# Blank idle matmuls, a later request for sixteen columns, and weights loaded by row halves, in the first norm of an encoder block

## The chip, the cores and the metric

The kernel runs on one core of a Trainium2 chip. The metric is device time in microseconds of one launch. The engines of the core: PE is TensorE (PEld its weight loads), DVE is VectorE, ACT is ScalarE, POOL is GpSimd, SP is SyncE, which here only issues DMAs.

## What is computed

One block of a hybrid encoder, in float32: `x` has 1024 tokens of 1024 channels, and 16 learned meta tokens stand ahead of them. The part that matters here is the beginning:

```python
h = jnp.concatenate([meta, x], axis=1)
u = rmsnorm(h, norm_mix)                      # y = x * rsqrt(mean(x*x) + 1e-6) * g
z = jnp.einsum('bld,dn->bln', u, w_in)        # w_in: 1024 x 4112
a, q, k, v, r, lr, ga, gb = jnp.split(z, IN_SPLITS, axis=-1)
log_a = log_sigmoid(lr @ w_gate_up + b_gate) / 16
```

`v` has 512 columns and the low-rank input `lr` has 16. Behind it come a multi-scale pooling mixer, a chunked gated linear attention over 4 heads, a merge by sigmoid gates, an output projection with a residual, a second rmsnorm, a squared-ReLU MLP of width 4096, and a last rmsnorm.

## The kernel before

**Arithmetic.** A product of two float32 matrices is taken as three products of rounded parts: each operand is split into a high part (ScalarE's Copy into the type fp32r) and a low part (VectorE's subtraction). `TH`/`TL` hold the high and low parts of the normed, transposed input, in two halves of 512 tokens; `w1h`/`w1l` and `vw` hold those of weights.

**The order of the work.** TensorE's instructions stand in the order in which the program writes them, everywhere (`manual_schedule` for PE around the whole run). In `start()`, the stage around the change, the order of ScalarE, VectorE and GpSimd is written out too. What lies outside that block on these engines, and SP's queue of DMAs, is ordered by a planner, which may bring instructions forward. Each engine works in order and stops at an instruction whose inputs aren't there.

**The first stage, `start()`.** x is taken in tiles of 128 tokens. SP asks for x's tile 0, the 128x128 identity (`ident`), the norm weights (`g8`), x's tile 1, two blocks of value weights (`fetch_vw(0)`, 512 KB each, into the two `raw` buffers), and tiles 2 and 3. GpSimd asks for the 16 low-rank columns of `w_in` (`lrraw`, L651). Later tiles are asked for when a buffer is free, in `normed()`.

A tile t goes through these steps:

- `squared(t)`, L606: ScalarE squares the tile and sums each row;
- `root(t)`, L608 and L609: ScalarE's Ln and Exp give a first estimate of the inverse root;
- `rest(t)`, L611 to L614 on VectorE (L611 and L616 to L619 on GpSimd from tile 3 on): one step that refines it;
- `normed(t)`, L660: VectorE scales the tile into `us`; then TensorE transposes its eight 128x128 blocks against the identity (L578) into two PSUM banks of four;
- `taken(t)`, twice, one bank each: VectorE multiplies by the norm weights into `ut` (L585), ScalarE makes the high part `th` (L594), and a returned function makes the low part `tl` on VectorE (L595).

`load_vw(0)` splits the value weights: `hi(j)` is ScalarE's high part of block j (L471), `lo(j)` VectorE's low part (L474), `lr()` the high part of the low-rank columns (L478, ScalarE), which returns the low part's function (L479, VectorE). `vw` holds 272 columns for each of 8 row blocks: 256 of values and 16 low-rank. In the kernel before, block j is 128 columns over all 1024 rows, in rows of 512 bytes.

`v_tile(0, t)` is the product of one tile with `vw`: "hh", "lh" and "hl", eight matmuls of 272 columns each (L506), one name for each pair of high and low parts. From tile 2 on the three are interleaved (L255 to L257).

`warm(n)` puts n idle transposes of the identity on TensorE (L668), into a bank that nothing reads; `WARM` holds the three counts. `S["fs"]` is a buffer that the gate stage uses later.

Of the kernel before, what the change touches and what calls it, by code (L numbers as in the profile page):

```python
# [11 lines left out]
ACT = mybir.ActivationFunctionType  # L12
ALU = mybir.AluOpType
AX = mybir.AxisListType

P = 128
D = 1024
SEQ = 1024
META = 16
KT = D // P  # L20
HALF = 512
# [9 lines left out]
NPAIR = DFF // P // 2  # L31
MP = 264
PACE, LEVEL = 1.1, 1.6
WARM = (4, 8, 12)


class Stack:
# [77 lines left out]
def kernel(  # L115
# [84 lines left out]
    def f32(ap):  # L200
        return ap.bitcast(F32)
# [245 lines left out]
    def w_cols(c):  # L447
        return w_in[:, c : c + P].rearrange("(k p) c -> p k c", p=P)
# [11 lines left out]
        return [slice(h * HALF, (h + 1) * HALF) for h in range(2)]  # L460

    def fetch_vw(i):
        return [raw.load(w_cols(C_V + i * 256 + j * P), D).rearrange("p (k c) -> p k c", k=KT) for j in range(2)]

    def load_vw(i, raws=None, parts=False):
        vw, raws = S["vw"][i], raws or fetch_vw(i)
        c = [slice(j * P, (j + 1) * P) for j in range(2)]
        eng = pool if i else dve

        def hi(j):  # L470
            act.activation(vw[:, 0, :, c[j]], raws[j], ACT.Copy)  # L471

        def lo(j):
            eng.tensor_tensor(vw[:, 1, :, c[j]], raws[j], f32(vw[:, 0, :, c[j]]), ALU.subtract)  # L474

        def lr():
            r = S["lrraw"]
            act.activation(vw[:, 0, :, 256:], r, ACT.Copy)  # L478
            return lambda: dve.tensor_tensor(vw[:, 1, :, 256:], r, f32(vw[:, 0, :, 256:]), ALU.subtract)  # L479

        if parts:
            return hi, lo, lr
        for j in range(2):
            hi(j)
            lo(j)
# [101 lines left out]
    def taken(b, t):  # L587

        half, at = t // 4, OFF[t // 4] + (t % 4) * P
        for j in range(2):  # L590
            ut = S["ut"][half, j][:, :, (t % 4) * P : (t % 4 + 1) * P]
            hi, lo = (a[half][:, 4 * j : 4 * j + 4, at : at + P] for a in (TH, TL))
            weighted(ut, b[j], j)
            act.activation(hi, ut, ACT.Copy)  # L594
            yield lambda lo=lo, ut=ut, hi=hi: dve.tensor_tensor(lo, ut, f32(hi), ALU.subtract)  # L595
# [26 lines left out]
    def start():  # L622
        act.preload_act_table_set("natural_log_exp_and_others")
        S["lrtok"] = left.push("lrtok", [P, 16, 16], F32)
        S["lrraw"] = left.push("lrraw", [P, KT, 16], F32)
        S["left_x"] = left.mark()
        xs = left.push("xs", [P, 4, D], F32)
        us = left.push("us", [P, 3, D], F32)
        xm = left.push("xm", [META, D], F32)
        g8 = xm[:KT, :P]  # L630
        mf = left.push("mf", [P, 6, CH], F32)
        S["u2p"] = right.push("u2p", [P, 2, HALF], F32)
        S["fs"] = right.push("fs", [P, 2, HALF], F32)
        S["s3"] = right.push("s3", [P, HALF], F32)
        q = gate_quarters
        q.lead = 1
        for i in range(2):
            q.places[i][0] = right.push(f"rawx{i}", [P, D], F32)
        S["right_ut"] = [right.mark()]
        S["ut"] = {}  # L640
        for half, j in ((0, 1), (1, 0), (1, 1), (0, 0)):
            S["ut"][half, j] = right.push(f"ut{half}{j}", [P, 4, HALF], F32)
            S["right_ut"].append(right.mark())
        S["vw"] = [right.push("vw0", [P, 2, KT, VP], F32R)]
        load = lambda t: nc.sync.dma_start(xs[:, t % 4], x[t * P : (t + 1) * P, :])
        load(0)
        nc.sync.dma_start(ident, ident_in)
        nc.sync.dma_start(g8, norm_mix.rearrange("(k p) -> k p", p=P))
        load(1)
        raws = fetch_vw(0)  # L650
        pool.dma_start(S["lrraw"], w_in[:, C_LR : C_LR + 16].rearrange("(k p) c -> p k c", p=P))  # L651
        load(2)
        load(3)
        m = lambda half, j: tuple(a[half][:, 4 * j : 4 * j + 4, OFF[half] : OFF[half] + HALF] for a in (TH, TL))
        q.x.update({"P1": m(0, 0), "P2": m(0, 1), "P3": m(1, 1)})
        run = S["gate_run"] = q.run()
        def normed(t):

            x_, u = of(t)
            dve.tensor_scalar(u, x_, rs[t], None, ALU.mult)  # L660
            if t < 4:
                load(t + 4)
            return turned(u)

        def warm(n):

            for _ in range(n):
                pe.transpose(idle[:, :P], ident, ident)  # L668

        idle = bank("x")  # L670
        of = lambda t: (xs[:, t % 4], us[:, t % 3])
        nothing = lambda: None
        with tc.manual_schedule(engines={mybir.EngineType.Activation, mybir.EngineType.DVE, mybir.EngineType.Pool}):
            rs, rms, b, leave = {}, {}, {}, None

            def squared(t):
                rms[t] = first_rms(xm if t == 8 else xs[:, t % 4], us[: META if t == 8 else P, t % 3], pool if t > 2 else dve)
                next(rms[t])

            def root(t):  # L680
                next(rms[t])

            def rest(t):
                rs[t] = next(rms[t])

            warm(WARM[0])
            bg = bank("ms")
            pe.transpose(bg[:, :KT], g8, ident[:KT, :KT])
            warm(WARM[1])
            squared(0)  # L690
            root(0)
            rest(0)
            b[0] = normed(0)
            dve.tensor_copy(gcol, bg[:, :KT])
            squared(1)
            root(1)
            lows = [list(taken(b[0], 0))]
            rest(1)
            warm(WARM[2])
            b[1] = normed(1)  # L700
            hi, lo, lr = load_vw(0, raws, True)
            hi(0)
            hi(1)
            lr_lo = lr()
            v0, leave0 = v_tile(0, 0, by_part=True)
            v1, leave = v_tile(0, 1, by_part=True)
            v0("hh")
            for fn in lows[0]:
                fn()
            v0("lh")  # L710
            lows.append(list(taken(b[1], 1)))
            v1("hh")
            for j in range(2):
                lo(j)
            lr_lo()
            v0("hl")
            squared(2)
            root(2)
            rest(2)
            b[2] = normed(2)  # L720
            v1("hl")
            for fn in lows[1]:
                fn()
            v1("lh")
            squared(3)
            root(3)
            rest(3)
            q.load(0, 0)
            squared(4)
            root(4)  # L730
            for t in range(1, 8):
                if t > 1:
                    left_now, leave = leave, v_tile(0, t, True)
                else:
                    left_now = leave0
                if t < 6:
                    b[t + 2] = normed(t + 2)
                if t < 2:
                    q.load(t, 0)
                elif t == 2:  # L740
                    nc.sync.dma_start(xm, meta)
                    q.load(0, 1)
                    q.load(1, 1)
                    nc.sync.dma_start(mf, masks)
                elif t == 7:
                    dve.tensor_scalar(xm, xm, rs[8], None, ALU.mult)
                for fn in left_now:
                    fn()
                if t < 6:
                    rest(t + 3)  # L750
                lows = list(taken(b[t + 1], t + 1)) if t < 7 else []
                if t < 5:
                    squared(t + 4)
                    root(t + 4)
                for fn in lows:
                    fn()
                for n in {5: (0,), 6: (1, 2), 7: (3,)}.get(t, ()):
                    q.prime(n == 0)
            differ((0, 0), (1, 0), (0, 0))
            bm = bank("ms")[:, : 8 * META].rearrange("p (a b) -> p a b", a=8)  # L760
            for i in range(KT):
                pe.transpose(bm[:, i], xm[:, i * P : (i + 1) * P], ident[:META, :META])
            um = us[:, 0, : 8 * META].rearrange("p (a b) -> p a b", a=8)
            for j in range(2):
                weighted(um[:, 4 * j : 4 * j + 4], bm[:, 4 * j : 4 * j + 4], j)
            th, tl = (a[0][:, :, :META] for a in (TH, TL))
            act.activation(th, um, ACT.Copy)
            dve.tensor_tensor(tl, um, f32(th), ALU.subtract)
            pool.tensor_copy(mask, mf)
            differences(run, leave)  # L770
# [1062 lines left out]
```

## Time and profile before

| | us |
|---|---|
| median of 3 runs | 1218.23 (1218.12 to 1218.29) |
| the profiled execution, its time | 1218.34 |
| its span, first to last instruction | 1216.1 |
| TensorE busy in the span | 1198.0 (99%) |
| VectorE / ScalarE / GpSimd busy | 854.6 / 618.5 / 63.0 |
| first TensorE instruction | 4.58 |

A row of the timeline gives start, duration, engine, line, operation, the tile written and the tiles read, shapes and, in brackets, how long the engine stood idle before it and what ended that wait. A row of the chain of waits gives start, duration, engine, tile and line of one piece of the chain that ended last. A row of the view of busy time by stretch gives the stretch, its length, the busy time and instruction count of PE, PEld, DVE, ACT and POOL, TensorE's granted clock, the DMA engines' mean busy share and GB/s. A row of a DMA queue gives packets, MB and the time that its packets took as a share of the 16 engines in the stretch asked for; `q1` is SP's queue and `q0` GpSimd's. A row of a DMA issue ends with KB and the time from issue to landing.

### The profile page before, as it was taken

Reading aid. Unit: us, or ns where it says so; the run is one execution under the profiler, and the core shown is the slowest. Engines: PE = TensorE matmul, PEld = TensorE weight load, DVE = VectorE, ACT = ScalarE, POOL = GpSimd, SP = SyncE. Lnnn points to the kernel's source line nnn. Section 1 sums busy time; section 2 is a strip of 40 time slices with the busy share of each in tenths; the row PEclk is TensorE's granted clock in tenths of the full one; section 3 lists DMA queues with packets and bytes.
Section 4 is the critical chain, followed back from the end, with each engine's and each line's share of the span. In section 5 each row is a group of like instructions: output and inputs, shape, how many; then the busy total and the mean of one; then the engine's idle time right before and its main releaser. Section 6 shows DMA issues by size and latency. Waiting matters only on the chain.

```text
span 1216.1 us, 18370 instructions
## 1 busy us (share of the span) xinstructions
PE 1198.0 (99%) x6818; PEld 997.9 (82%) x6818; DVE 854.6 (70%) x1411; ACT 618.5 (51%) x1103; POOL 63.0 (5%) x100
## 2 busy tenths in 40 slices
PE   7999999999999999999999999999999999999997
PEld 7878888988887778888888888888888888888886
DVE  7996676654556677735897667676675887887686
ACT  7667567322446663324655455454554444444554
POOL 2000000001201126000000000000000000000000
PEclk9999999999999999999999999999999999999999
DMA  8043426146102246741245454344479973333532
GB/s 255 2 113 114 125 77 201 45 153 223 36 19 62 71 144 230 267 149 70 105 139 166 145 165 156 130 162 146 168 239 326 337 241 96 95 98 94 173 96 87
DMA packets 141672, 173.84 MB, mean 143 GB/s; under 512 B 9944, under 2 KB 81392, under 8 KB 141584
## 3 DMA queue, kind: packets, MB, share of 16 engines
q1 hardware_dynamic: 141552, 172.62, 44.0%
q8 instruction: 53, 0.87, 0.3%
q14 instruction: 35, 0.29, 0.1%
q0 software_dynamic: 32, 0.07, 0.1%
HBM read 119.17 MB, written 53.48 MB: 142 GB/s over the span
## 4 chain that ended last, share of the span: by engine, by line
PE 92%; DVE 4%; ACT 2%; issue 1%; DMA 0%; POOL 0%; SPq 0%; ACTq 0%; POOLq 0%; DVEq 0%
PE b_mm L255 11%; PE b_mm L256 11%; PE b_mm L257 11%; PE b_ms L257 9%; PE b_ms L255 9%; PE b_ms L256 9%; PE b_x L256 8%; PE b_x L255 8%; PE b_x L257 8%; PE b_mx L255 1%; PE b_sc L1227 1%; PE b_mx L256 1%; PE b_mx L257 1%; PE b_ms L1505 1%; DVE ut L783 1%
## 5 line engine op out<-in xcount | busy, mean ns | idle before, releaser
L255 PE MATMUL b_mm<-th,w1h 128*128 128x512 f32 (+1 forms) x312 | 117.6, 377 | 1.1 <-DVE c L818 1.0
L256 PE MATMUL b_mm<-tl,w1h 128*128 128x512 f32 (+1 forms) x312 | 115.9, 372 | 0.0
L257 PE MATMUL b_mm<-th,w1l 128*128 128x512 f32 (+1 forms) x312 | 115.9, 371 | 0.0
L255 PE MATMUL b_x<-th,w1h 128*128 128x512 f32 (+1 forms) x240 | 90.8, 378 | 0.0
L256 PE MATMUL b_x<-tl,w1h 128*128 128x512 f32 (+1 forms) x240 | 90.7, 378 | 0.0
L257 PE MATMUL b_x<-th,w1l 128*128 128x512 f32 (+1 forms) x240 | 90.3, 376 | 0.0
L273 ACT ACTIVATE w1h<-raw 128x512 fp32r<-128x512 f32 x96 | 59.5, 620 | 29.0 <-PE b_ms L256 13.7
L274 DVE TENSOR_TENSOR w1l<-raw,w1h 128x512 fp32r<-128x512 f32 x96 | 65.6, 684 | 8.6 <-ACT w1h L273 8.6
L255 PEld LDWEIGHTS b_mm<-th,w1h 128*128 128x128 f32 x312 | 58.6, 188 | 12.5 <-issue 1.9
L273 ACT ACTIVATE w1h<-fs 128x512 fp32r<-128x512 f32 x72 | 45.3, 631 | 44.9 <-PE b_ms L256 30.8
L257 PEld LDWEIGHTS b_mm<-th,w1l 128*128 128x128 f32 x312 | 58.6, 188 | 10.4
L256 PEld LDWEIGHTS b_mm<-tl,w1h 128*128 128x128 f32 x312 | 58.6, 188 | 9.8
L273 ACT ACTIVATE w1h<-bt 128x512 fp32r<-128x512 f32 x44 | 27.8, 632 | 67.1 <-issue 62.7
L274 DVE TENSOR_TENSOR w1l<-fs,w1h 128x512 fp32r<-128x512 f32 x72 | 49.2, 686 | 15.0 <-ACT w1h L273 14.9
L1681 DVE TENSOR_TENSOR bt<-w,w 128x512 f32<-128x512 f32 x80 | 54.7, 684 | 1.6 <-DMA w<-in_w_ff_dram 1.6
L257 PEld LDWEIGHTS b_x<-th,w1l 128*128 128x128 f32 x240 | 45.1, 188 | 8.5
L255 PEld LDWEIGHTS b_x<-th,w1h 128*128 128x128 f32 x240 | 45.1, 188 | 8.4
L256 PEld LDWEIGHTS b_x<-tl,w1h 128*128 128x128 f32 x240 | 45.1, 188 | 8.3
L273 ACT ACTIVATE fxh<-bt 128x512 fp32r<-128x512 f32 x36 | 22.8, 632 | 55.7 <-issue 50.1
L257 PE MATMUL b_ms<-wo,w1l 128*128 128x512 f32 x128 | 49.9, 390 | 0.0
L255 PE MATMUL b_ms<-wo,w1h 128*128 128x512 f32 x128 | 49.8, 389 | 0.0
L256 PE MATMUL b_ms<-wo,w1h 128*128 128x512 f32 x128 | 49.8, 389 | 0.0
(455 smaller groups left out, 3345.2 us busy)
## 6 DMA issues: line engine op xcount, KB each, us to landing
hf_dram<-h SPq DMA_DIRECT2D x112, 256.0 KB, 2.1
raw<-hf_dram SPq DMA_DIRECT2D x112, 256.0 KB, 2.7
w<-in_w_ff_dram SPq DMA_DIRECT2D x64, 256.0 KB, 4.8
raw<-in_w_in_dram SPq DMA_DIRECT2D x24, 512.0 KB, 4.8
raw<-in_w_ff_dram SPq DMA_DIRECT2D x16, 512.0 KB, 4.1
rawx<-in_w_ff_dram SPq DMA_DIRECT2D x16, 512.0 KB, 4.0
xs<-in_x_dram SPq DMA_DIRECT2D x8, 512.0 KB, 5.5
rawx<-in_w_in_dram SPq DMA_DIRECT2D x8, 512.0 KB, 4.4
```

The costliest lines, as they stand in the source:

```text
L255: pe.matmul(ps, ah, bh, start=first and i == 0, stop=False, skip_group_check=more)
L256: pe.matmul(ps, ah, bl, start=False, stop=False, skip_group_check=more)
L257: pe.matmul(ps, al, bh, start=False, stop=last and i == n - 1, skip_group_check=more)
L273: act.activation(hi, a, ACT.Copy)
L274: dve.tensor_tensor(lo, a, f32(hi), ALU.subtract)
L783: dve.tensor_tensor(to_, a_, b_, ALU.subtract)
L1227: pe.matmul(b[to, e, j], kk[r, s], qq[r, s], start=True, stop=True, tile_position=(e * CH, u * CH))
L1505: pe.transpose(b[j][:, i], u[:, (4 * j + i) * P : (4 * j + i + 1) * P], ident)
L1681: dve.tensor_tensor(bt, w, S["w2"][q[3:]][:, i], ALU.add if q[2] == "+" else ALU.subtract)
```

## The change

The idle work on TensorE is a float32 matmul of a blank tile with itself: the first 128 columns of `S["fs"]`, which VectorE sets to zero. It needs no load. `WARM` has four counts: ten ahead of the transposition of the norm weights, four behind it, two ahead of tile 1's transposes, and three behind the splits of the value weights.

The low-rank columns are asked for by GpSimd behind a copy of one column of x's tile 1 into the same buffer, so behind that tile's landing.

The value weights come as two row halves of 512 rows by 256 columns (rows of 1 KB), and `hi(j)`, `lo(j)` work on row blocks 4j to 4j+3. This holds for the second set (`load_vw(1)`) too.

The second half of tile 0's `taken` (L585 and L594) moves behind tile 1's `rest` and `normed` on VectorE and behind `hi(0)` on ScalarE; `lr()` stands ahead of `hi(1)`.

```diff
-WARM = (4, 8, 12)
+WARM = (10, 4, 2, 3)
...
     def fetch_vw(i):
-        return [raw.load(w_cols(C_V + i * 256 + j * P), D).rearrange("p (k c) -> p k c", k=KT) for j in range(2)]
+        rows = lambda j: w_in[j * HALF : (j + 1) * HALF, C_V + i * 256 : C_V + (i + 1) * 256]
+        return [raw.load(rows(j).rearrange("(k p) c -> p k c", p=P), D).rearrange("p (k c) -> p k c", k=4) for j in range(2)]
...
-        c = [slice(j * P, (j + 1) * P) for j in range(2)]
+        at = lambda n, j: vw[:, n, 4 * j : 4 * j + 4, :256]
...
-            act.activation(vw[:, 0, :, c[j]], raws[j], ACT.Copy)
+            act.activation(at(0, j), raws[j], ACT.Copy)
...
-            eng.tensor_tensor(vw[:, 1, :, c[j]], raws[j], f32(vw[:, 0, :, c[j]]), ALU.subtract)
+            eng.tensor_tensor(at(1, j), raws[j], f32(at(0, j)), ALU.subtract)
...
         raws = fetch_vw(0)
-        pool.dma_start(S["lrraw"], w_in[:, C_LR : C_LR + 16].rearrange("(k p) c -> p k c", p=P))
...
+        blank = S["fs"][:, 0, :P]
+        dve.memset(blank, 0.0)
+
         def warm(n):
 
             for _ in range(n):
-                pe.transpose(idle[:, :P], ident, ident)
+                pe.matmul(idle[:, :P], blank, blank, start=True, stop=True)
...
+            pool.tensor_copy(S["lrraw"][:, 0, :1], xs[:, 1, :1])
+            pool.dma_start(S["lrraw"], w_in[:, C_LR : C_LR + 16].rearrange("(k p) c -> p k c", p=P))
             warm(WARM[0])
...
-            lows = [list(taken(b[0], 0))]
+            parts = taken(b[0], 0)
+            lows = [[next(parts)]]
             rest(1)
             warm(WARM[2])
             b[1] = normed(1)
             hi, lo, lr = load_vw(0, raws, True)
             hi(0)
+            lows[0] += parts
+            lr_lo = lr()
             hi(1)
-            lr_lo = lr()
+            warm(WARM[3])
```

## Prediction

> **What bounds the kernel now.** The profile page's first line, then the view of busy time by stretch, for two stretches.
>
> ```profile
> span 1216.1 us, 18370 instructions
> ```
>
> ```profile
> 24.00:1180.00 1156.00, 1151.88 (x6578) 958.65 (x6577) 814.95 (x1327) 585.29 (x1030) 57.47 (x82) 1.00 0.44 142
> 1180.00:1216.10 36.10, 28.37 (x126) 23.13 (x124) 24.19 (x54) 16.48 (x37) 0.00 (x0) 0.93 0.26 88
> ```
>
> From 24 us to 1180 us TensorE (first busy column) is idle for 1156.00 - 1151.88 = 4.1 us. What starts sooner or later ahead of 24 us shifts all of that and comes out in the total nearly one for one, and the stake is small. The change works ahead of 24 us, so I read that stretch in the chain of waits:
>
> ```profile
> 2.07 6.04 DMA xs<-in_x_dram
> 8.13 1.16 ACT us L606 x2
> ...
> 10.86 0.75 DVE us L660
> ...
> 13.45 1.23 ACT th L594 x2
> ...
> 16.18 1.14 ACT us L606 x2
> ...
> 19.72 0.76 DVE us L660
> ...
> 22.52 0.39 PE b_mm L257
> ```
>
> The end is set by x's second tile (asked for at 2.07, landed at 8.1), its norm, then from 13.45 by ScalarE, in order: split of tile 1 (L594), squares of tiles 2 and 3 (L606), the norm of tile 3 on GpSimd, VectorE, and TensorE from 22.5 on. So one start decides: **L594 at 13.45**. The timeline has what stands before it (rows of TensorE, VectorE and ScalarE, in this order):
>
> ```profile
> 7.59 1.91 PE L578 MATMUL b_ms<-ident,us 128*128 128x128 f32 x8
> ...
> 11.66 1.09 PE L578 MATMUL b_ms<-ident,us 128*128 128x128 f32 x8 [0.77 <-DVE us L660]
> ...
> 8.69 0.69 DVE L585 TENSOR_TENSOR ut<-b_ms,small 128x512 f32<-128x512 f32 x1 [1.21 <-PE b_ms L578]
> 9.54 0.69 DVE L585 TENSOR_TENSOR ut<-b_ms,small 128x512 f32<-128x512 f32 x1 [0.16 <-PE b_ms L578]
> 10.15 0.14 DVE L611 TENSOR_SCALAR small<-small 128x1 f32<-128x1 f32 x1
> 10.41 0.22 DVE L613 SCALAR_TENSOR_TENSOR small<-small 128x1 f32<-128x1 f32 x1
> ...
> 11.52 1.29 DVE L595 TENSOR_TENSOR tl<-ut,th 128x512 fp32r<-128x512 f32 x2
> 12.73 1.28 DVE L585 TENSOR_TENSOR ut<-b_ms,small 128x512 f32<-128x512 f32 x2
> ...
> 9.31 0.29 ACT L608 ACTIVATE small<-small 128x1 f32<-128x1 f32 x1
> 9.64 0.20 ACT L609 ACTIVATE small<-small 128x1 f32<-128x1 f32 x1
> ...
> 10.80 1.99 ACT L471 ACTIVATE vw<-raw 128x1024 fp32r<-128x1024 f32 x2
> 12.70 0.29 ACT L478 ACTIVATE vw<-lrraw 128x128 fp32r<-128x128 f32 x1
> 13.45 1.23 ACT L594 ACTIVATE th<-ut 128x512 fp32r<-128x512 f32 x2 [0.46 <-DVE ut L585]
> ```
>
> Eight transposes take 1.91 us at 7.59 and 1.09 at 11.66: TensorE's pace changes in between. VectorE waits 1.21 us for the first group, and from 10.86 it is full. L594 waits for tile 1's L585 at 12.73; the low-rank columns (L478) are split at 12.70 without a wait.
>
> **The change, part by part.**
>
> *Idle matmuls.* A blank tile needs one memset. Rows of the timeline (VectorE's first, TensorE's first), then pieces of the chain of waits:
>
> ```profile
> 0.81 0.07 DVE L1191 MEMSET metab<- 128x16 f32 x1 [0.81 <-PEq L1822]
> 4.58 1.11 PE L668 MATMUL b_x<-ident 128*128 128x128 f32 x4 [4.58 <-DMA ident<-in_ident_dram]
> ```
>
> ```profile
> 37.19 0.45 PE b_ms L578 x4
> 37.66 0.70 DVE ut L585
> ...
> 388.25 1.03 PE b_m L1316 x32
> ```
>
> After a memset of that size TensorE starts near 1.1 instead of 4.58, 3.5 us sooner. The eight transposes that end at 9.50 are the last at the lower pace, 4.9 us after TensorE's first work, so the pace should now rise by 6.0, if TensorE stays busy. Full f32 matmuls on a 128x128 tile aren't in the trace: L1316's smaller ones take 1.03/32 = 0.03 us each, the idle transposes 1.11/4 = 0.28; between those ends I take 0.28, the row of the same shape. Ten then end at 1.1 + 2.8 = 3.9, and four behind the identity (4.58) and the norm weights well before tile 0's transposes at 7.5. At the fast pace VectorE follows 0.47 behind four transposes (37.19 to 37.66), so L585 starts at 7.59 + 0.47 = 8.06 instead of 8.69: **-0.6**, bounds 0 (the hole of 0.7 us or more until the identity lands keeps the pace down) and -0.6. The two and three further matmuls lie in TensorE's wait for L660.
>
> *Order on VectorE.* The second half of tile 0's L585 moves behind L660 of tile 1. L660 then waits only for L613's inputs, and the half's own 0.69 is worked off after it. A gain only if x's second tile comes early enough; on its own it costs.
>
> *The low-rank request.* Rows of DMA, by stretch: GpSimd's queue in 3.5:4.5, 4.5:6 and 6:7, then the landings of x's second tile, of the low-rank columns and of the second value-weight block (issued 2.94), and rows of GpSimd, and one of VectorE, in the timeline:
>
> ```profile
> q0 software_dynamic: 16, 0.06, 65.2%
> q0 software_dynamic: 13, 0.01, 1.9%
> q0 software_dynamic: 3, 0.00, 0.2%
> ...
> xs<-in_x_dram SPq DMA_DIRECT2D x1, 512.0 KB, 6.0
> lrraw<-in_w_in_dram POOLq DMA_DIRECT2D x1, 64.0 KB, 5.7
> raw<-in_w_in_dram SPq DMA_DIRECT2D x1, 512.0 KB, 8.6
> ```
>
> ```profile
> 1.27 1.10 POOL L651 DMA_DIRECT2D lrraw<-in_w_in_dram  x1 [0.44 <-issue]
> ...
> 17.77 1.29 DVE L595 TENSOR_TENSOR tl<-ut,th 128x512 fp32r<-128x512 f32 x2
> ...
> 18.02 0.48 POOL L616 TENSOR_TENSOR small<-small 128x1 f32<-128x1 f32 x1
> ...
> 20.87 0.19 POOL L617 TENSOR_TENSOR small<-small 128x1 f32<-128x1 f32 x1
> ```
>
> In 3.5 to 4.5 the low-rank columns held 65% of all 16 engines for 1 us, just ahead of x's second tile. Without them that tile lands 0.65 sooner: 8.13 - 0.65 = 7.48, bounds 8.13 (the value weights take the room) and 7.0.
>
> The path by VectorE: squares end 1.15 after landing, 8.65; L608 8.68, L609 9.01, end 9.21; L585 (first half) 8.06 to 8.74; L613 9.24, L660 0.45 later (10.41 to 10.86), 9.69; second half of L585 0.66 later (10.86 to 11.52), 10.35; two L595 0.69 later, 11.04; tile 1's L585 1.21 later (11.52 to 12.73), 12.25; L594 0.72 later (12.73 to 13.45): **12.97**, i.e. -0.48. With the tile at 7.0 the first L585's end, 8.75, limits (L611 to L660 0.71): -0.71. With it at 8.13 (L613 9.87): +0.15.
>
> What was moved must still land. GpSimd now waits for x's tile, runs a one-column copy (0.19, up to 0.48 beside VectorE's L595), then the request: 7.48 + 0.3 = 7.8. Behind it on GpSimd stands nothing that is needed before the norm of tile 3 (L616 at 18.02). The copy is one more reader of the tile's buffer, but the next load into that waits for L660 anyway. From issue to landing it took 5.7, the data packets being over by 5.0 (3.7 after the issue); 13 of 16 closing packets were out by 6.0, three later. Bounds 3.7 and 5.7; I take 5.0, since the last three belong to engines that lagged in the stretch where x's tile was also late, and the request now begins when that tile is whole. Landing 12.8. And L478 has moved ahead of the second L471, so ScalarE, in order, holds behind it: the second L471, both L594, the squares of tiles 2 and 3. From L478's start to L594 it is 0.26 + 0.95 = 1.21 (12.70 to 12.96; half of L471's pair). So L594 at 12.8 + 1.21 = 14.01: **+0.56**, in place of the -0.48 by VectorE; the later of the two counts. With 3.7 the landing is 11.5, L594 12.7 by this path, and VectorE's 12.97 stands. With 5.7: 13.5, +1.26. The landing costs from 11.8 on and is worse than before from 12.24 on.
>
> By the Trainium skill, "DMA: Bandwidth & Descriptors", section "Anatomy of one DMA — SWDGE (gpsimd) path", a request from GpSimd costs about 2.0 us plus bytes over 436 GB/s, 2.15 for these 64 KB; with the 1.10 of the issue that would land at 11.05 and the wait would vanish. The row here (5.7) speaks against it.
>
> *Value weights by row halves.* Same bytes in 1 KB rows instead of 512 B. The second block landed at 2.94 + 8.6 = 11.54 before; its L471 is now due near 12 at the earliest (second half of L585 to 11.04, its L594, then L478), so it isn't last. TensorE's first products can begin on half the rows, but what ends their stage is the low part of the low-rank columns on VectorE, as before: nothing. SP spends less on descriptors; x's later tiles aren't in the chain. The second set of value weights is fetched far inside the stretch where TensorE is full: nothing; uncovered, a block's landing would show, 8.6 us at the worst row here.
>
> *Sum.* 1218.34 (the profiled execution: span 1216.1 and 2.2 around it) + 0.56 = 1218.9; the median of the runs, 1218.23, lies 0.11 lower: **1218.8**.
>
> **Rivals.**
> 1. *The columns land in time* (by 11.8). For it: data packets over 3.7 us after the issue. Against: SP's queue, by then, is fuller (row below, 7 to 9 us: 122.6%) than in the stretch where the 5.7 was measured. -0.48 (to -0.71): 1217.8.
>
> ```profile
> q1 hardware_dynamic: 1222, 0.65, 122.6%
> ...
> 13.04 1.27 PE L506 MATMUL b_mm<-vw,th 128*128 128x272 f32 x8 [0.29 <-ACT vw L478]
> ```
>
> 2. *It doesn't do what it says*: pace and x's tile unchanged. Landing 8.13 + 0.3 + 5.0 = 13.4, L594 at 14.6, +1.2: 1219.4.
> 3. *GpSimd is slowed by VectorE while it writes the request* — the slower side. L616 took 0.48 beside VectorE's L595, L617 0.19 beside its L585: 2.5 times. In the run before the request was written with VectorE idle; now VectorE is busy from 8.06 on, though with L585 first, which weighs against it. 1.10 and the 1.2 to the first data packet (2.37 to 3.5) become 2.8 and 3.0, landing 14.5 (the issue alone) to 16.3: +2.3 to +4.1, about +3.0: 1221.2. It leaves the 0.2% from a landing at 14.64 on, +2.4. The Trainium skill, "SBUF — State Buffer", the box on the "DVE blocks DMA" trap, says that VectorE in a two-port mode locks GpSimd out of writing descriptors; the rows here show slower GpSimd operations and no locked request.
> 4. *The planner sets another order later*: L1191, of a much later stage, ran at 0.81, so order outside the written-out part is its own choice. At most the 4.1 us that TensorE idles, either way: 1214 to 1222.
> 5. *TensorE falls back to the lower pace* with fewer idle matmuls after 9 us: three passes like the one at 13.04 above, 1.2 each, would take double: +3.5: 1221.7.
>
> **How the numbers follow.** Forecast (late by under 1.5 us): 0.42. Rival 1: 0.27. Rival 2: 0.08. Rival 3: 0.10, 0.08 of it beyond +2.4. Rival 4: 0.10, of which 0.04 faster and 0.04 slower by over 0.2%. Rival 5: 0.03. A measurement of this kernel tells about 0.2%, 2.4 us, from no change. Faster 0.04; slower 0.08 + 0.04 + 0.03 = 0.15; within 0.81. The range takes forecast, rivals 1 and 2 and the near parts of 3 and 4 (0.81): from 1217.4 (-0.71, with 0.1 for runs) to 1220.7; the forecast's own is 1218.3 to 1219.7.
>
> **What would show it.** TensorE at work from about 1.1 us; tile 0's transposes in about 1.1 us, not 1.91; L585 at 8.1; x's squares of tile 1 at 7.5; GpSimd's request near 7.8; a wait on ScalarE in front of L478 named after the columns' DMA, of about 1 us; L594 near 14.0. No wait there and L594 at 13.0 means rival 1; a request row well over 1.10 is rival 3; a shift that appears only behind 60 us is rival 4. The forecast is wrong if L594's shift and the end's shift differ by over 0.5 us.

## The result and the profile after

The changed kernel takes **1220.45 us** (median of 14 runs, 1220.09 to 1221.77) against 1218.20 for the kernel before on the same chip (14 runs, 1217.74 to 1218.65): ratio 1.0019, 95% interval 1.0012 to 1.0027, so 2.25 us slower. The profiled execution, of which the rows below are, is the longest of the 14: 1221.77, that is 3.43 above the profiled one of before.

The changed kernel's page and its view of busy time by stretch:

```profile
span 1219.7 us, 18402 instructions
```

```profile
24.00:1180.00 1156.00, 1151.58 (x6591) 959.31 (x6591) 814.29 (x1325) 585.52 (x1032) 58.25 (x84) 1.00 0.44 142
```

TensorE is idle for 4.42 us between 24 and 1180 us, against 4.1 before: hardly anything changed there. The 3.6 us by which the span grew lie ahead of it. The chain of waits of the changed kernel:

```profile
2.04 5.72 DMA xs<-in_x_dram
...
7.82 0.20 POOL lrraw L689
8.02 0.29 issue
8.30 6.52 DMA lrraw<-in_w_in_dram
...
14.91 0.32 ACT vw L479
...
15.27 7.09 PE b_mm L507 x32
22.36 0.87 PE b_ms L579 x8
```

Of VectorE's and ScalarE's norm work nothing is left in it. It runs from x's second tile to GpSimd's copy, the request, 6.52 us of transfer, the split of the columns, and then TensorE's products. Most lines of the changed kernel are numbered one higher: L594 is L595 now, L478 is L479, L471 is L472, L585 is L586, L578 is L579, L606 is L607, L506 is L507. Its timeline (TensorE, VectorE, ScalarE, GpSimd, in this order):

```profile
1.05 4.11 PE L671 MATMUL b_x<-fs 128*128 128x128 f32 x20 [1.05 <-DVE metab L1199]
7.52 1.09 PE L579 MATMUL b_ms<-ident,us 128*128 128x128 f32 x8 [1.11 <-DVE us L660]
11.72 0.83 PE L671 MATMUL b_x<-fs 128*128 128x128 f32 x6
15.27 2.22 PE L507 MATMUL b_mm<-vw,th 128*128 128x272 f32 x8 [2.72 <-ACT vw L479]
...
8.21 0.69 DVE L586 TENSOR_TENSOR ut<-b_ms,small 128x512 f32<-128x512 f32 x1 [0.67 <-PE b_ms L579]
12.64 1.28 DVE L586 TENSOR_TENSOR ut<-b_ms,small 128x512 f32<-128x512 f32 x2
...
7.79 1.06 ACT L607 ACTIVATE us<-xs 128x1024 f32<-128x1024 f32 x1 [1.56 <-DMA xs<-in_x_dram]
14.91 0.31 ACT L479 ACTIVATE vw<-lrraw 128x128 fp32r<-128x128 f32 x1 [2.91 <-DMA lrraw<-in_w_in_dram]
15.13 1.04 ACT L472 ACTIVATE vw<-raw 128x1024 fp32r<-128x1024 f32 x1
16.07 1.14 ACT L595 ACTIVATE th<-ut 128x512 fp32r<-128x512 f32 x2
...
7.82 0.19 POOL L689 COPY lrraw<-xs 128x1 f32<-128x1 f32 x1 [6.74 <-DMA xs<-in_x_dram]
8.30 1.11 POOL L690 DMA_DIRECT2D lrraw<-in_w_in_dram  x1 [0.30 <-POOL lrraw L689]
```

Each of the intended steps is there: TensorE at work from 1.05, tile 0's transposes in 1.09, L586 at 8.21, x's second tile a little sooner (7.79). VectorE begins tile 1's L586 at 12.64, where it began at 12.73 before. But ScalarE stands for 2.91 us in front of L479, and L595, whose start decided the end before, starts at 16.07 instead of 13.45: **+2.62**. The end moved by 3.6, which is 1.0 more than L595, and the chain above doesn't pass through L595 any more: from L479 it goes by TensorE's products. The view of busy time by stretch, last columns TensorE's granted clock, DMA share and GB/s, shows what happens there:

```profile
12.00:14.00 2.00, 0.55 (x5) 0.36 (x4) 1.97 (x4) 0.00 (x0) 0.00 (x0) 1.00 1.04 330
14.00:15.00 1.00, 0.00 (x0) 0.00 (x0) 1.00 (x1) 0.09 (x1) 0.00 (x0) 0.85 0.98 339
15.00:21.00 6.00, 5.73 (x25) 5.73 (x26) 3.73 (x9) 5.87 (x13) 0.98 (x2) 0.50 0.64 171
```

While ScalarE waits TensorE has nothing either (0.55 us of work from 12 to 14, none from 14 to 15), and its clock falls to 0.50 for the six microseconds in which the first products run: eight take 2.22 us instead of 1.27.

### The profile page after: what moved, and what is told of

Its sections match the earlier page's. It is cut to its first block, busy times and chain, and to the rows that moved or that the text cites. A ratio compares the mean times of both kernels' runs of the same rounds, so it can differ in the third digit from the quotient of the medians.

```text
span 1219.7 us, 18402 instructions
## 1 busy us (share of the span) xinstructions
PE 1200.9 (98%) x6832; PEld 1002.1 (82%) x6832; DVE 855.5 (70%) x1412; ACT 618.6 (51%) x1103; POOL 63.4 (5%) x101
## 4 chain that ended last, share of the span: by engine, by line
PE 90%; DVE 5%; ACT 2%; DMA 1%; issue 1%; SPq 0%; POOL 0%; ACTq 0%; DVEq 0%
PE b_mm L255 11%; PE b_mm L256 11%; PE b_mm L257 11%; PE b_ms L256 9%; PE b_ms L255 9%; PE b_ms L257 9%; PE b_x L256 8%; PE b_x L255 8%; PE b_x L257 8%; PE b_mx L255 1%; PE b_sc L1235 1%; PE b_mx L256 1%; PE b_mx L257 1%; PE b_mm L507 1%; DVE w1l L274 1%
## 5 line engine op out<-in xcount | busy, mean ns | idle before, releaser
L274 DVE TENSOR_TENSOR w1l<-fs,w1h 128x512 fp32r<-128x512 f32 x72 | 49.3, 686 | 15.0 <-ACT w1h L273 14.9
```

Source lines behind the costliest of these rows:

```text
L274: dve.tensor_tensor(lo, a, f32(hi), ALU.subtract)
```

## The experiments

All times stand beside runs of the kernel before on the same chip: eleven runs of each version, fourteen of the change and seven of "request on ScalarE's queue". In the table, the shift of tile 1's high part (L594 or L595) and of the span are those of one profiled execution each, against 13.45 and 1216.1.

| run | median (range), us | kernel before | ratio, 95% interval | shift of tile 1's high part | shift of span |
|---|---|---|---|---|---|
| the change | 1220.45 (1220.09-1221.77) | 1218.20 | 1.0019 [1.0012, 1.0027] | +2.62 | +3.6 |
| request early | 1218.37 (1217.62-1218.84) | 1218.35 | 0.9998 [0.9990, 1.0007] | +0.33 | +0.4 |
| request on SP | 1217.32 (1217.04-1217.65) | 1218.35 | 0.9992 [0.9983, 1.0001] | -0.66 | -0.7 |
| only request late | 1219.75 (1218.94-1221.31) | 1218.35 | 1.0012 [1.0003, 1.0021] | +1.51 | +2.0 |
| long filler | 1220.19 (1219.67-1221.93) | 1218.35 | 1.0017 [1.0008, 1.0026] | +2.20 | +1.8 |
| pace kept | 1219.81 (1219.47-1220.67) | 1218.31 | 1.0012 [1.0003, 1.0021] | +2.14 | +2.3 |
| columns split later | 1218.55 (1218.08-1220.11) | 1218.31 | 1.0003 [0.9994, 1.0012] | +0.66 | +2.0 |
| request on ScalarE's queue | 1221.80 (1220.22-1223.73) | 1218.31 | 1.0027 [1.0016, 1.0038] | +2.64 | +2.7 |
| queue held back | 1217.67 (1217.15-1218.20) | 1218.49 | 0.9994 [0.9985, 1.0002] | -0.50 | -0.8 |
| idle matmuls only | 1217.63 (1217.28-1219.51) | 1218.31 | 0.9998 [0.9989, 1.0006] | -0.49 | -0.6 |
| rows only | 1218.45 (1217.90-1219.21) | 1218.49 | 1.0001 [0.9992, 1.0010] | +0.15 | +0.4 |
| SP request alone | 1217.84 (1217.11-1218.66) | 1218.49 | 0.9995 [0.9986, 1.0004] | +0.02 | -0.1 |
| idle matmuls and SP request | 1217.42 (1216.97-1218.47) | 1218.49 | 0.9991 [0.9983, 1.0000] | -0.78 | -0.6 |

The theory is that the late columns hold ScalarE, and with it tile 1 (A in the expectations that use letters). Its first rival is that TensorE's lost pace is the price (B there), its second that the other edits cost something by themselves (C).

### The request: back, elsewhere, alone

*Request early*: the changed kernel with GpSimd's request at the start, as before.

```diff
-            pool.tensor_copy(S["lrraw"][:, 0, :1], xs[:, 1, :1])
-            pool.dma_start(S["lrraw"], w_in[:, C_LR : C_LR + 16]...)
...
         raws = fetch_vw(0)
+        pool.dma_start(S["lrraw"], w_in[:, C_LR : C_LR + 16]...)
```

> The changed kernel with one part undone: GpSimd asks for the low-rank columns at the start, without the copy behind x's tile 1. Theory A (the columns land late and ScalarE holds behind them): the wait of 2.91 us ahead of L479 in the changed kernel is gone, x's tile 1 lands at about 8.1 again, tile 1's high part starts at 13.6 or sooner (13.45 before, 16.07 in the changed kernel), and the time is 1217.8 to 1218.6. Rival B (TensorE's lower pace from 15 to 21.6 us is the cost by itself, brought by the fewer idle matmuls): the pace still falls, and the time stays above 1219.5. Rival C (idle matmuls, order on VectorE or row halves cost by themselves): the time stays above 1219.

*Request on SP*: the same, but asked for on SP's queue between x's second tile and the value weights (`nc.sync.dma_start` ahead of `raws = fetch_vw(0)`).

> The changed kernel with the request moved to SP's queue, directly behind x's tile 1 and ahead of the value weights, without a copy. Theory A: x's tile 1 lands at about 7.8 as in the changed kernel, the columns by 10 us, no wait ahead of the split of the low-rank columns, tile 1's high part at 12.7 to 13.1, time 1217.4 to 1218.0. Rival C: above 1219.

*Only request late*: the kernel before, with the copy and the late request of the change and nothing else of it.

> The kernel before with only the request moved behind x's tile 1 (copy and all), everything else as before; the low-rank split stands behind both value-weight splits there. Theory A: the columns land at 14.5 to 15, a wait of about 2 us ahead of the split at 12.7, tile 1's high part at 15.0 to 15.3, time 1219.7 to 1220.5. Rival C: under 1218.6, since the request itself would cost nothing.

The late request by itself costs 1.40 us, and without it the other edits cost nothing (0.02) or, with the request on SP, gain 1.03, at an interval that just reaches 1. (Line numbers in these kernels differ by a few, as lines were added or taken out.) The timeline of "only request late" (ScalarE) and its DMA rows:

```profile
14.74 0.31 ACT L478 ACTIVATE vw<-lrraw 128x128 fp32r<-128x128 f32 x1 [2.25 <-DMA lrraw<-in_w_in_dram]
14.96 1.14 ACT L594 ACTIVATE th<-ut 128x512 fp32r<-128x512 f32 x2
```

```profile
lrraw<-in_w_in_dram POOLq DMA_DIRECT2D x1, 64.0 KB, 6.3
```

The same kind of hold, 2.25 us, comes with the old order and no blank matmuls. From the split of the columns to tile 1's high part it is 0.22 here (14.74 to 14.96), and 1.16 in the change (14.91 to 16.07), whose new order puts the second L472 behind the wait too. Of the 1.11 by which the change's high part is later than this one, 0.94 is that order, the rest a later landing. And the timeline of "request on SP" (SP's queue, then ScalarE):

```profile
2.43 0.43 SPq L651 DMA_DIRECT2D lrraw<-in_w_in_dram  x1
...
6.87 1.06 ACT L607 ACTIVATE us<-xs 128x1024 f32<-128x1024 f32 x1 [0.76 <-DMA xs<-in_x_dram]
11.34 0.29 ACT L479 ACTIVATE vw<-lrraw 128x128 fp32r<-128x128 f32 x1
12.79 1.23 ACT L595 ACTIVATE th<-ut 128x512 fp32r<-128x512 f32 x2 [0.21 <-DVE ut L586]
```

No wait in front of L479, tile 1's high part at 12.79, and x's second tile at 6.87: on SP's queue the columns stay out of that tile's way and still land in time.

### Is it TensorE's pace?

*Long filler* and *pace kept* are the changed kernel with more idle matmuls: `WARM = (10, 4, 2, 14)` and `WARM = (10, 4, 10, 15)` for `(10, 4, 2, 3)`.

> The changed kernel with 14 idle matmuls in place of 3 ahead of the first products, 3.1 us at 0.22 each, so that TensorE is at work until the columns land; the request stays late. Theory A: the wait ahead of L479 stays at 2.5 to 3 us and tile 1's high part near 16; the granted clock stays at 1.00 between 15 and 22 us; the time is 1220.0 to 1220.5, so the pace explains only what the profiled execution (1221.77) had over the median (1220.45). Rival B: with the pace kept the time falls under 1219.2.

> The changed kernel with idle matmuls (10, 4, 10, 15): the ten fill TensorE's hole from 8.5 to 10.7 us, the fifteen the time until the columns land. (The run with fourteen at the end and two before tile 1 had lost the pace at 11.8 us already, in the hole ahead of tile 1's transposes, and its filler ran until 16.6, past the landing, so it did not part the two theories.) Theory A (late columns hold ScalarE): granted clock 1.00 from 8 to 22 us, the wait ahead of L479 still 2 to 3 us, tile 1's high part at 15.6 to 16.1, time 1219.9 to 1220.5. Rival B (the lower pace is the cost): under 1219.2.

"Long filler" told nothing: the clock fell right behind an earlier hole (TensorE idle for 1.89 us up to 11.03, clock 0.50 from 11.8 to 15), so its matmuls ran at half pace and past the columns' landing, until TensorE came to the products at 16.63. "Pace kept" fills that hole too. Its timeline and busy time by stretch:

```profile
14.42 0.31 ACT L479 ACTIVATE vw<-lrraw 128x128 fp32r<-128x128 f32 x1 [2.93 <-DMA lrraw<-in_w_in_dram]
15.59 1.14 ACT L595 ACTIVATE th<-ut 128x512 fp32r<-128x512 f32 x2
```

```profile
15.00:21.00 6.00, 5.64 (x45) 5.23 (x44) 3.91 (x8) 5.84 (x13) 1.38 (x3) 1.00 0.71 172
```

Full clock throughout, the same wait of 2.93, and still +1.50 us: the wait is the larger part of the price. The difference to the change's +2.25, about 0.75, is an estimate of what the lost pace is worth, and no more: the ranges of the two versions overlap, and in the two profiled executions the columns landed at different times (14.4 here, 14.8 there). Within the change's own fourteen executions the time doesn't follow the mean granted clock either: 1220.82 us at 0.999, 1220.10 at 0.995. Here the shifts of tile 1 (+2.14) and of the span (+2.3) agree again.

*Columns split later* takes the hold off ScalarE and leaves the columns late: "pace kept", with `lr()`, and the first products that need it, behind tile 1's high parts.

```diff
-            lr_lo = lr()
             hi(1)
...
-            v0("hh")
             for fn in lows[0]:
                 fn()
-            v0("lh")
             lows.append(list(taken(b[1], 1)))
+            lr_lo = lr()
+            v0("hh")
+            v0("lh")
```

> As e8_pace_kept, but the split of the low-rank columns stands behind tile 1's high parts on ScalarE, so that only tile 2's squares and the first products wait for the columns. Theory A1 (the price is ScalarE's order: tile 1's high parts behind the wait): tile 1's high part back at 13.0 to 13.5, tile 2's squares at 15.2 instead of 17.1, the time between, 1218.9 to 1219.4. Theory A2 (the price is the first products on TensorE, which cannot start before the columns): no better than e8_pace_kept, 1219.9 or more.

Its timeline (ScalarE, then TensorE):

```profile
8.54 1.06 ACT L607 ACTIVATE us<-xs 128x1024 f32<-128x1024 f32 x1 [2.44 <-DMA xs<-in_x_dram]
...
14.11 1.23 ACT L595 ACTIVATE th<-ut 128x512 fp32r<-128x512 f32 x2 [0.41 <-DVE ut L586]
15.79 0.31 ACT L479 ACTIVATE vw<-lrraw 128x128 fp32r<-128x128 f32 x1 [0.45 <-DMA lrraw<-in_w_in_dram]
...
16.15 1.27 PE L507 MATMUL b_mm<-vw,th 128*128 128x272 f32 x8 [0.17 <-ACT vw L479]
```

The median is 1.26 lower than that of "pace kept" on the same chip: ten of its eleven runs are below all eleven of that one, and lower than either theory expected. So most of the price lies in what stands behind the late landing on ScalarE. The profiled execution is the eleventh, the longest (1220.11): x's tile came at 8.54, the columns were split at 15.79, and there the end moved by 2.0 while tile 1's high part moved by 0.66. Its chain of waits runs from the columns straight to the products at 16.15, so a landing that late costs by TensorE as well. Where the columns landed in the ten shorter executions isn't recorded.

### Why do the columns take 6.5 us?

*Request on ScalarE's queue*: the changed kernel without the copy, the request issued by ScalarE behind the squares of tile 1.

> The changed kernel with the request issued by ScalarE's own DMA queue behind the squares of x's tile 1 (the same moment, some 9.0 us, no copy), so that no descriptors are written by GpSimd. If the 5.9 to 6.5 us from issue to landing are GpSimd's (its writing of the request, or its queue): landing 3.5 to 4.5 after the issue, at 12.5 to 13.5, wait ahead of the split about 1.5, time 1218.8 to 1219.5. If they come from the full DMA engines (100% busy by SP's queue from 8 to 15 us): 6 us again, landing at 15 or later, time 1220.5 or more. The issue itself takes 0.4 us of ScalarE in either case.

Its DMA rows, the columns' issue and then the two hardware queues from 10 to 11 and from 13 to 14 us (`q10` is ScalarE's):

```profile
lrraw<-in_w_in_dram ACTq DMA_DIRECT2D x1, 64.0 KB, 8.0
```

```profile
q1 hardware_dynamic: 109, 0.40, 98.8%
q10 hardware_dynamic: 44, 0.00, 3.0%
...
q1 hardware_dynamic: 82, 0.30, 83.7%
q10 hardware_dynamic: 442, 0.03, 30.3%
```

Issued at 6.91, 1.4 us ahead of the change's request, and without GpSimd, the columns landed at 14.9, where the change's landed at 14.8. So a late landing doesn't need GpSimd's way of asking. None of their packets passes from 7 to 10; in the fourth microsecond behind the issue they get 3% of the DMA engines' time while SP's queue has 98.8%, and ten times as many pass three microseconds later. The two transfers aren't alike, though: ScalarE's queue carries the columns in 1040 packets, GpSimd's in 32. The next run keeps the transfer and changes the backlog.

*Queue held back*: the changed kernel with x's tiles 2 and 3 asked for only behind GpSimd's request; a copy into tile 2's place, on GpSimd, holds SP back, and with them tile 4, which SP asks for next.

```diff
         raws = fetch_vw(0)
-        load(2)
-        load(3)
...
             pool.dma_start(S["lrraw"], w_in[:, C_LR : C_LR + 16]...)
+            pool.tensor_copy(xs[:, 2, :1], xs[:, 1, :1])
+            load(2)
+            load(3)
```

> The changed kernel with the request where it is, at 7.8 to 8.9 on GpSimd, but x's tiles 2 and 3 are requested only behind it, after GpSimd has written a column of tile 2's place, so that SP's queue holds 1 MB less while the columns are under way. Theory that SP's full queue makes the late request land 6.5 after its issue: the columns land 4 to 5 after the issue, at 12 to 13, the wait ahead of L479 falls from 2.9 to between 0 and 1, tile 1's high part begins at 13 to 14, and the time falls to 1218.2 to 1219.2, unless tile 2 itself then comes late (its squares begin at 17.1 now; its load should land at 14 to 15). Rival, that a request issued at this time takes 6.5 of itself on GpSimd's path: landing at 14.5 again, the wait 2.5 to 3, 1219.8 to 1220.5.

Its timeline (SP, GpSimd, ScalarE) and its DMA rows, the columns' issue and the queues from 7.9 to 11.1 us:

```profile
9.20 1.80 SPq L646 DMA_DIRECT2D xs<-in_x_dram  x4
...
7.86 1.11 POOL L688 DMA_DIRECT2D lrraw<-in_w_in_dram  x1 [0.30 <-POOL lrraw L687]
...
11.49 0.29 ACT L479 ACTIVATE vw<-lrraw 128x128 fp32r<-128x128 f32 x1
12.95 1.23 ACT L595 ACTIVATE th<-ut 128x512 fp32r<-128x512 f32 x2 [0.21 <-DVE ut L586]
```

```profile
lrraw<-in_w_in_dram POOLq DMA_DIRECT2D x1, 64.0 KB, 3.2
...
q1 hardware_dynamic: 452, 0.54, 64.0%
q0 software_dynamic: 32, 0.07, 16.5%
```

And the change's row of SP's requests for x, and its queues over the same length behind the columns' request, 8.3 to 11.5 us:

```profile
3.46 7.75 SPq L646 DMA_DIRECT2D xs<-in_x_dram  x4
...
q1 hardware_dynamic: 614, 1.33, 106.5%
```

The same request by the same engine at nearly the same time lands after 3.2 us instead of 6.5; the wait is gone and the time is 1217.67, with an interval that doesn't touch the change's. In the change, not one packet of GpSimd's queue passes in those 3.2 us. Three of the four requests in its row, for tiles 2, 3 and 4 at 3.46, 4.01 and 7.54, stand ahead of the columns' at 8.30; in "queue held back" all four stand behind it. The late request pays for these 1.5 MB of x, which are needed later than the columns.

### The other parts alone

*Idle matmuls only*: the kernel before with the blank matmuls, `WARM = (10, 4, 6)`. *Rows only*: with the row halves alone. *SP request alone*: with `nc.sync.dma_start` for the columns ahead of the value weights alone. *Idle matmuls and SP request*: with these two.

> The kernel before with only the blank idle matmuls, WARM (10, 4, 6), all else as before. By the changed kernel's trace (tile 0's transposes in 1.09 us, L585 at 8.2): VectorE's first-half product at 8.2 instead of 8.69, the second half by 9.4, so L611 waits for the squares and no more for VectorE; tile 1's scaling at 10.3 instead of 10.86; time 0.4 to 0.6 shorter, 1217.6 to 1217.9. Rival: the lead is lost again to x's tile 1 landing at 8.1, 1218.1 to 1218.4.

> The kernel before with one part of the change alone: the first value weights come by row halves, 1 KB a piece, and their high and low parts are made by row halves. Prediction's claim for this part: nothing, 0.0 us, since both halves were landed at 11.3 and their first use on ScalarE is at 11.56. If the rows did bring something, it would show as the halves landing some 1 us sooner (the changed kernel's landed 6.7 and 7.7 after issue instead of 8.6) and so as a lighter queue for whatever lands beside them, x's second tile above all. Time expected: 1218.3, from 1218.0 to 1218.6, no step in the first 25 us moved by more than 0.2.

> The kernel before with the request for the low-rank columns alone moved: on SP's queue, directly behind x's second tile and ahead of the value weights. If a request that stands ahead of the 2 MB of value weights and x tiles in the queue lands in time whoever issues it, the columns land at about 7.5, ScalarE has no wait at L478, and x's second tile, freed of the 1.8 us early request of GpSimd, lands at 7 to 8 instead of 8.13. Time expected: 1217.9, from 1217.5 to 1218.3. If it was GpSimd's early issue that kept the queue short in the kernel before, the value weights land later and the time rises to 1218.5 or more.

> The kernel before with blank idle matmuls from the start and the request on SP's queue directly behind x's second tile; no row halves, and the old order on ScalarE. It asks whether the gain of the changed kernel with the request on SP (1217.3) needs the other parts. If the two edits make it by themselves: 1217.4, from 1217.0 to 1217.8. If the row halves or the new order carry a part of it: 1217.8 to 1218.2.

ScalarE's rows in the timelines of "SP request alone", then of "idle matmuls and SP request":

```profile
7.05 1.06 ACT L606 ACTIVATE us<-xs 128x1024 f32<-128x1024 f32 x1 [0.90 <-DMA xs<-in_x_dram]
13.47 1.23 ACT L594 ACTIVATE th<-ut 128x512 fp32r<-128x512 f32 x2 [0.47 <-DVE ut L585]
```

```profile
6.85 1.06 ACT L606 ACTIVATE us<-xs 128x1024 f32<-128x1024 f32 x1 [0.67 <-DMA xs<-in_x_dram]
12.67 1.23 ACT L594 ACTIVATE th<-ut 128x512 fp32r<-128x512 f32 x2 [0.46 <-DVE ut L585]
```

The tile 1 us sooner brings L594 nothing while tile 0's transposes still run at the low pace (1.92 us; L594 at 13.47, against 13.45); with the blank matmuls it starts at 12.67. The row halves bring nothing (-0.04 us; in the profiled execution TensorE's first work came 0.29 later, more than the 0.2 that was expected at most). The two edits alone gain 1.07, as much as "request on SP" (1.03), so the row halves and the new order aren't needed for the gain. That gain is about 1 us, and the interval of every one of these versions reaches 1, so none is shown to be faster than the kernel before. "Request on SP" is the best that was run, some 3 us below the change.

## Why the prediction came out as it did

**The bound** was right: what moved ahead of 24 us came out in the total, and TensorE's idle time behind it did not change. In the eight versions that kept TensorE's clock and the columns ahead of tile 1, the shift of tile 1's high part and that of the span agree within 0.3 us.

**Idle matmuls.** Right in effect: transposes in 1.09 us, L585 at 8.21 where 8.06 was forecast, and alone they gave 12.96 for L594. That this is the figure of the path by VectorE (12.97) is luck: the sum held the new order and a tile at 7.48, this run the old order and a tile at 7.64. In the changed kernel VectorE came to tile 1's L586 at 12.64, not 12.25; 0.3 of that is the tile, the rest its L596, which waits for the moved half of tile 0. The price of one was too low: 4.11 us for ten, 0.41 each, not 0.28. The first ten ended at 5.2 instead of 3.9, still 2.4 ahead of the transposes.

**x's second tile** was forecast 0.65 sooner and was 0.34 sooner in the profile (7.79 against 8.13). It is not a fixed shift: over the profiled executions it started at 7.64 to 8.21 (four kernels) with GpSimd's early request, at 6.90 to 8.54 (seven) with a late one, at 6.85 to 7.05 (three) with SP's. Each kernel was profiled once, so this is a spread and not a mean; only with SP's request is the tile some 1 us sooner in every one.

**The low-rank request** is the step that failed in size. Its mechanism was forecast and is there: ScalarE in order, L479 ahead of the second L472, tile 1 behind both. In the profiled execution L595 came 2.06 later than forecast: 0.28 from the tile (whole at 7.76), 0.24 from the copy and the gap behind it (request 0.54 behind the tile, not 0.3), and 1.52 from the landing. **The landing was taken as 5.0 us, with 5.7 as its upper bound, and took 6.52.** The bound was a landing of the kernel before, for a request at 1.27, when SP had put less into its queue. That the queue would be fuller at 8 us stood in the text, as an argument against rival 1 only; it belonged in the term itself. "Queue held back" shows both ends: 3.2 us with the queue thin, 6.5 with it full. By the Trainium skill, "DMA: Bandwidth & Descriptors", section "Anatomy of one DMA — SWDGE (gpsimd) path", with the issue's 1.10 added, the estimate was 3.25; the thin queue here agrees with it (3.2), the full one took 3.3 us more.

**TensorE's pace**, rival 5, had 0.03 and came true as well in the profiled execution, in a smaller size and for a cause that the text didn't name: not too few idle matmuls after 9 us as such, but the hole that the forecast's own wait made. Its price was given as 3.5; it is 1.0 in the profiled execution and, as an estimate, about 0.75 by the medians. It is why the end moved by 1.0 more than L595, which the prediction had set as the sign that its sum is wrong.

**The other rivals.** Rival 3, GpSimd slowed while writing the request, is refuted: 1.11 us with VectorE at work from 8.21 to 8.90, against 1.10 before. Nor is the later start of the data VectorE's doing: in "queue held back" it was at work beside the request too (8.26 to 8.95), and the columns landed after 3.2. Rival 1's landing came only with SP's queue held back. Rival 4 has nothing behind 24 us to show for it. Row halves: nothing, as forecast.

In sum: direction and carrying wait right, +0.56 forecast, +2.25 measured. The time is inside the range, 0.25 from its upper end, and the ratio just inside the 0.2% called no change, though its interval leaves 1 out. That is luck in part: the forecast's own range, up to 1219.7, misses the time by 0.75, and the upper end that holds it was drawn for the near parts of rivals 3 and 4, not for a landing of 6.5. If about 0.75 is the pace, the rest, 0.9 more than forecast, is the mis-sized landing. How the two divide in the typical run, and not in the longest one profiled, stays open.

## What to carry to other kernels

Ask of a transfer that is moved back what the other queues have asked for by then: here 64 KB that were needed soon waited behind 1.5 MB that were needed later, and asking from ScalarE in place of GpSimd didn't help. Put it on the busy queue itself, at the place where its turn is due, or hold the later loads back. And take a landing time for a bound only from a stretch with the same load on the DMA engines; a wait put into an in-order engine can be paid again where TensorE loses its clock in the hole, as in the profiled execution here.

## What the runs showed of the hardware

- A request that met a full queue of another engine landed at 14.4 to 15.7 us in six kernels, whether issued at 6.91 by ScalarE or between 7.75 and 9.1 by GpSimd: the issuer didn't set the landing, and with the backlog held back it came at 11.1. By the Trainium skill, "DMA: Bandwidth & Descriptors", section "Queues, rings and completion order", each DMA engine takes turns between queues packet by packet. The rows here, counted in packets, don't show equal turns: none of ScalarE's queue beside 837 of SP's from 7 to 10 us, 44 beside 109 in the next microsecond, 442 beside 82 from 13 to 14; none of GpSimd's beside 614 in 3.2 us. What holds the packets back at first is not settled by these runs.
- A full float32 matmul of 128x128 shows as two instructions: ten give a row of x20. It took 0.41 us among the first ten and 0.28 later (three in a row of x6, 0.83). The view gives a granted clock of 1.00 for both, so it doesn't show the lower pace of TensorE's first microseconds, which the transposes of the kernel before (1.91 us, then 1.09) show as well. In "long filler" the view does give 0.50, and 13 such instructions take 2.95 us there.
- TensorE's granted clock fell to 0.50 at holes of 2.72 (the change), 2.81 ("only request late"), 3.00 ("request on ScalarE's queue") and, in "long filler", 1.89 us. Holes of 2.02 ("request early", up to 11.22) and 1.73 (the change, up to 10.79), both ahead of the second transposes, left it at 1.00. Length alone doesn't decide it.
